# Turning the 32x32 blocks of a triangular inverse on VectorE instead of TensorE, in the recurrent part of a diffusion layer

## The chip, the cores and the metric

The kernel runs on one core of one Trainium2 chip. The metric is device time in microseconds, from the first to the last instruction of one execution and the little that lies around it. The time of before is the median of three runs.

## The reference, cut to what matters

One layer of a hybrid backbone is applied to 128 prompt tokens and 512 sample tokens (640 columns in all). A combined input projection feeds a differential attention, a recurrent branch that runs over the tokens in both directions, and gates. A residual normalisation and a convolutional feed-forward block follow. The recurrent branch is what the change is about:

```python
def rwkv7_scan(s0, r, w, k, v, a, b, reverse):
    def step(S, inp):
        r_t, w_t, k_t, v_t, a_t, b_t = inp
        sa = jnp.einsum('bhvk,bhk->bhv', S, a_t)
        S = S * w_t[:, :, None, :] + sa[..., None] * b_t[:, :, None, :] + v_t[..., None] * k_t[:, :, None, :]
        return S, jnp.einsum('bhvk,bhk->bhv', S, r_t)
    s_final, ys = lax.scan(step, s0, xs, reverse=reverse)
```

There are 8 heads of 64, two directions, and 640 tokens. The final states of the prompt are an output (`new_s`).

## The kernel before, in words

The scan is done in chunks of 64 tokens: 10 chunks, 2 directions. Heads go in pairs, `i` = 0 to 3, and a pair has 2 heads x 2 directions x 10 chunks = 40 small systems. Each is a unit lower triangular 64x64 matrix that has to be inverted. The tile `MS` holds all 40 of a pair, with the 64 rows on partitions 0 to 63; partitions 64 to 127 hold other products.

One pair goes through these functions, which issue their work in the order written:

- `rw_b(i)` makes decays, keys and queries (VectorE, ScalarE, GpSimd); it is a generator, and is stepped from within `rw_m(i - 1)`.
- `rw_c(i)` multiplies keys with queries (L642) and masks the products into `MS` (L648, L651, VectorE).
- `rw_d(i)`, a generator, transposes values and keys and makes `UV` (L665, L677, L686, with evacuations on ScalarE).
- `rw_i(i)` inverts the two 32x32 diagonal blocks of each of the 40 systems. TensorE turns the blocks so that a system lies on a partition: 64 small matmuls against the identity (L706; the profile lists two instructions for each, 128 a pair) into PSUM, and four copies (L710) into `X`, whose 104 partitions are 40 systems' first blocks, 24 unused rows, and 40 systems' second blocks. Then 30 steps of forward substitution run on VectorE, each a product (L716) and a sum (L718). Then `X` is turned back by 8 transposes of TensorE (L729) and 16 copies (L733, 8 on VectorE, 8 on ScalarE) into `MS`.
- `rw_m(i)` joins the blocks (a transpose by VectorE, L741, and small matmuls L747, L755), turns, solves and joins the chunk transitions (`turned`, `solved`, `joined`: L777, L792, L813, L816) in ten iterations, with the chain of states in `step` (L839). At its end it turns the final states `FS` (L864), copies them out (L865) and stores them (L867).
- `rw_e(i)` makes the outputs (L888) and copies them out of PSUM (`y`, L889). `rw_f(i)`, a generator, normalises and gates them (L899 to L923) and stores them (L925).

PSUM banks for all of this come from `bank(psR, "m", 2)`, two banks in turn.

In between, TensorE is given products of the combined input projection, which do not depend on the recurrence: the generator `flow` yields one dense product at a time (L215, 128x128 weights, 320 columns), 38 blocks of 48 products after those done at the start, 1824 in all. `pull(n)` issues `n` of them. Weights are loaded by SyncE (L183), cast by ScalarE (L186), and their low part is taken by GpSimd (L187). `side()` steps the first generator in the list `sides` until it is finished, then the next. While `order[0]` is set, all of TensorE's instructions of this part are chained in the order in which they are issued. What is left of `flow` after `rw_f(3)` is issued in one go (`while pull(1)`).

After that comes attention: its loads of queries and keys (L1097) stand behind the store of `rw_f(3)` (L925) in SyncE's queue, and its first matmuls are L1116.

Of the kernel before, what the change touches and what calls it, by code (L numbers as in the profile page):

```python
# [11 lines left out]
F32 = mybir.dt.float32  # L12
F32R = mybir.dt.float32r
AF = mybir.ActivationFunctionType
ALU = mybir.AluOpType
# [3 lines left out]
P = 128  # L19
# [47 lines left out]
def tile_layer(ctx, tc, x_prompt, x_sample, cache_k, cache_v, state_rwkv, c, c_ctx, w_ada, b_ada, w_in,  # L67
# [4 lines left out]
    nc = tc.nc  # L72
    def chain(prev, bi):
        if prev is not None:
            tc.add_manual_dep(bi.ins, prev.ins.name,
                              mybir.DependencyInfo(mybir.DependencyClass.NoSync, mybir.DependencyReason.DATA),
                              reason="psum group order")
        return bi
# [114 lines left out]
    def pq(bi):  # L193

        if order[0]:
            order[1] = chain(order[1], bi)
        return bi
# [60 lines left out]
    def bank(pool, tag, bufs=1):  # L258
        return pool.tile([P, 512], F32, name="ps_" + tag, tag=tag, bufs=bufs)
# [18 lines left out]
    with tc.tile_pool(name="start", bufs=1) as sp, tc.tile_pool(name="psS", bufs=2, space=PSUM) as psS:  # L278
# [95 lines left out]
        prev = None  # L374
# [78 lines left out]
    def side(n=1):  # L453

        while sides and n:
            n -= 1
            if next(sides[0], None) is None:
                del sides[0]

    def need(i, key):  # L460
        while key not in R[i] and pull(1):
# [231 lines left out]
    def rw_i(i):  # L693
        MS = R[i]["MS"]

        X = rp.tile([104, 32, 32], F32, name="X", tag="st")
        tmp = rp.tile([104, 256], F32, name="tmpx", tag="tmpx")
        nc.gpsimd.memset(X[32:64], 0.0)
        prev = None

        for y in range(2):
            ps = bank(psR, "m", 2).rearrange("p (t s) -> p t s", s=32)
            for t in range(16):
                for b in range(2):
                    rows = slice(32 * b, 32 * b + 32)
                    prev = chain(prev, pq(nc.tensor.matmul(ps[64 * b:64 * b + 40, t, :], MS[rows, :, 32 * b + 16 * y + t], ident[rows, rows], start=True, stop=True)))  # L706
                if t % 8 == 7:
                    pull(6)
            for b in range(2):
                (nc.scalar.copy if b else nc.vector.tensor_copy)(out=X[64 * b:64 * b + 40, 16 * y:16 * y + 16, :], in_=ps[64 * b:64 * b + 40])  # L710
        Xf = X.rearrange("p t s -> p (t s)")
        nc.vector.memset(Xf[:, ::33], 1.0)
        for j in range(1, 31):
            n = 31 - j
            tv = tmp[:, 0:j * n].rearrange("p (t r) -> p t r", r=j)
            nc.vector.tensor_tensor(out=tv, in0=X[:, j:j + 1, 0:j].broadcast_to([104, n, j]),  # L716
                                    in1=X[:, j + 1:32, j:j + 1].broadcast_to([104, n, j]), op=ALU.mult)
            nc.vector.tensor_tensor(out=X[:, j + 1:32, 0:j], in0=X[:, j + 1:32, 0:j], in1=tv, op=ALU.add)  # L718
            side()
            pull(4)  # L720
        while "d_in" not in R[i]:
            side()
            pull(4)

        for y in (1, 0):
            ps = bank(psR, "m", 2)
            for u in (3, 2, 1, 0):
                c0 = 128 * (4 * y + u)
                prev = chain(prev, pq(nc.tensor.transpose(out=ps[:, 104 * u:104 * u + 104], in_=Xf[:, c0:c0 + 128], identity=ident[0:104, 0:104])))  # L729
            for q in range(4):  # L730
                for b in range(2):
                    t0 = 32 * b + 16 * y + q
                    (nc.scalar.copy if b else nc.vector.tensor_copy)(  # L733
                        out=MS[32 * b:32 * b + 32, :, t0:t0 + 13:4],
                        in_=ps[32 * q:32 * q + 32, 0:416].rearrange("p (u r) -> p r u", u=4)[:, 64 * b:64 * b + 40, :])
        pull(16)

    def rw_m(i):
        AR, BT, UV, gs, st_in, MS = (R[i][k] for k in ("AR", "BT", "UV", "gs", "st_in", "MS"))
# [103 lines left out]
        for v in range(10):  # L843
            put = turned(v + 1) if 0 < v < 4 else None
            if v == 0:
                turned(0)()
                pull(10)
                put = turned(1)
            if 1 <= v <= 5:
                joined(v - 1)  # L850
            if v < 5:
                solved(v)
            if put:
                put()
            if v > 2:
                s = v - 3
                step([(d, cc, ST[:, d, cc + 1 - 2 * d, :]) for d, cc in ((0, 2 + s), (1, 9 - s))] +
                     ([(0, 1, FS[:, 0, :]), (1, 0, FS[:, 1, :])] if v == 7 else []))
            side(3)
            pull(14)  # L860
        ps = bank(psR, "m", 2)
        fo = rp.tile([64, 2, P], F32, name="fo", tag="tmpx")
        for d in range(2):
            pq(nc.tensor.transpose(out=ps[0:64, d * P:(d + 1) * P], in_=FS[:, d, :], identity=ident))  # L864
        nc.scalar.copy(out=fo, in_=ps[0:64, 0:256].rearrange("p (d k) -> p d k", d=2))  # L865
        for d in range(2):
            nc.sync.dma_start(out=new_s[d, 2 * i:2 * i + 2].rearrange("e v k -> v e k"), in_=fo[:, d, :].rearrange("p (e k) -> p e k", e=2))  # L867

        R[i].update(UV=UV, ST=ST)

    def rw_e(i):
        AR, MS, UV, ST = (R[i][k] for k in ("AR", "MS", "UV", "ST"))
        gup = cb.tile([P, P], F32, name="gup", tag="gup", bufs=1)
        nc.sync.dma_start(out=gup, in_=rw_g_up[:, i * P:(i + 1) * P])

        y = ft("y")
        for c0, n in ((0, 2), (2, 8)):
            ps = bank(psR, "m", 2)

            vals = [(d, cc, 0) for cc in range(c0, c0 + n) for d in range(2)]  # L880
            states = [(d, cc, 1) for cc in range(c0, c0 + n) for d in range(2) if (d, cc) not in ((0, 0), (1, 1))]
            todo = vals + states
            prev = None
            for z, (d, cc, kind) in enumerate(todo):
                for e in range(2):
                    hs = slice(64 * e, 64 * e + 64)
                    w, x = (ST[hs, d, cc, :], AR[d][hs, cc, 1, :]) if kind else (UV[:, e, d, cc, :], MS[:, e * 20 + d * NCH + cc, 64:128])
                    prev = chain(prev, pq(nc.tensor.matmul(ps[hs, (cc - c0) * 64:(cc - c0) * 64 + 64], w, x, start=z == 0, stop=z == len(todo) - 1)))  # L888
            nc.scalar.copy(out=y[:, c0 * 64:(c0 + n) * 64], in_=ps[:, 0:n * 64])  # L889
        R[i].update(y=y, gup=gup)  # L890

    def rw_f(i):
        v, bon, gup, y = (R[i][k] for k in ("v", "bon", "gup", "y"))
# [142 lines left out]
    for i in range(4):  # L1036
        if i:
            rw_e(i - 1)
        rw_c(i)
        need(i, "v_in")  # L1040
        sides.append(rw_d(i))
        if i:
            sides.append(rw_f(i - 1))
        rw_i(i)
        if i < 3:
            need(i + 1, "rk_in")
            sides.append(rw_b(i + 1))
        rw_m(i)
        while sides:
            side()  # L1050
            pull(3)
# [544 lines left out]
```

## Time and profile before

| | |
|---|---|
| time, median of 3 runs | 1432.46 us (1431.22 to 1436.12) |
| the profiled execution's own time | 1437.26 us |
| its span | 1435.2 us |
| mean granted clock of TensorE | 0.932 of 2.4 GHz |
| TensorE matmul busy | 1287.7 us (90%) |
| VectorE busy | 911.8 us (64%) |
| ScalarE, GpSimd busy | 563.7 us, 564.9 us (39% each) |

The profile is of one execution; its span ends with the last instruction, and 2.1 us of its time lie around it. Busy TensorE time is modelled from pipelined matmuls, so two dense products that are each listed with 0.31 us can start 0.15 us apart. A row of the timeline is: start, duration (both us), engine, line, operation, output<-inputs, shape, count, and in brackets the idle time of the engine just before and what ended it. The recurrent part lies between 69 and 711 us of the span.

### The profile page before, as it was taken

What the parts mean: (1) busy time and instruction counts of PE and PEld (TensorE: products, weight loads), DVE (VectorE), ACT (ScalarE), POOL (GpSimd) and SP (SyncE); (2) the same over time, 40 slices, a digit from 0 to 9 for tenths busy, and PEclk for the clock granted to TensorE, in tenths of its full rate; (3) what the DMA queues carried; (4) which work ended last, traced back from release to release, by engine and by line L of the source; (5) the groups of instructions that cost most, each with busy time, mean ns of one, the idle gap of its engine ahead of it and who ended that gap; (6) DMA issues with size and microseconds to landing.
All of it is one profiled execution on the core that took longest, in us unless ns stands there. A gap on an engine that the chain in (4) does not pass through costs nothing.

```text
span 1435.2 us, 27691 instructions
## 1 busy us (share of the span) xinstructions
PE 1287.7 (90%) x11105; PEld 1140.6 (79%) x11105; DVE 911.8 (64%) x1683; ACT 563.7 (39%) x1158; POOL 564.9 (39%) x424
## 2 busy tenths in 40 slices
PE   6998898988888999999979889968999999999994
PEld 5887887877777888889867777758988989989983
DVE  2365847584847563831266523597897987778777
ACT  3442533344324441533355412354543433434432
POOL 3252217331643232212220235546654735536623
PEclk9997998898988998999989999978999999999997
DMA  9411212220222111212656787513232232322222
GB/s 306 125 49 34 63 30 69 78 76 28 64 72 70 51 33 51 77 50 75 195 160 204 265 265 265 171 60 102 74 104 73 74 96 66 90 66 79 69 67 88
DMA packets 157459, 144.64 MB, mean 101 GB/s; under 512 B 10490, under 2 KB 128020, under 8 KB 157332
## 3 DMA queue, kind: packets, MB, share of 16 engines
q1 hardware_dynamic: 147490, 127.85, 29.0%
q10 hardware_dynamic: 9842, 15.03, 3.1%
q8 instruction: 87, 1.43, 0.4%
q14 instruction: 40, 0.33, 0.1%
HBM read 121.06 MB, written 19.69 MB: 98 GB/s over the span
## 4 chain that ended last, share of the span: by engine, by line
PE 38%; DVE 16%; issue 5%; POOL 4%; ACT 3%; DMA 2%; SPq 0%; ACTq 0%; DVEq 0%; POOLq 0%
PE ps_d L1413 8%; PE ps_d L215 6%; PE ps_x L215 4%; PE ps_e L1413 3%; PE acc L1449 2%; PE acc L1447 2%; PE acc L1448 2%; DVE sums L1386 2%; DVE zacc L1462 1%; PE acc L1249 1%; PE T L1140 1%; POOL wl L224 1%; DMA ws<-in_w_out_dram 1%; DVE X L718 1%; DVE tmpx L716 1%
## 5 line engine op out<-in xcount | busy, mean ns | idle before, releaser
L187 POOL TENSOR_TENSOR wl<-ws,wh 128x512 fp32r<-128x512 f32 x100 | 138.5, 1386 | 400.5 <-ACT wh L186 349.4
L224 POOL TENSOR_TENSOR wl<-sums,wh 128x512 fp32r<-128x512 f32 x88 | 137.4, 1568 | 38.3 <-ACT wh L223 36.5
L1413 PE MATMUL ps_d<-oph,wh 128*128 128x320 f32 x440 | 138.5, 315 | 10.6 <-DVE u L1425 5.0
L224 POOL TENSOR_TENSOR wl<-wu,wh 128x512 fp32r<-128x512 f32 x63 | 88.9, 1412 | 142.9 <-ACT wh L223 129.6
L1413 PE MATMUL ps_d<-oph,wl 128*128 128x320 f32 x440 | 137.5, 313 | 0.6 <-POOL wl L224 0.6
L1413 PE MATMUL ps_d<-opl,wh 128*128 128x320 f32 x440 | 137.3, 312 | 0.7 <-DVE opl L224 0.7
L186 ACT CAST wh<-ws 128x512 fp32r<-128x512 f32 x100 | 61.4, 618 | 171.3 <-PE ps_d L215 66.9
L215 PE MATMUL ps_x<-hl,wh 128*128 128x320 f32 (+1 forms) x304 | 104.5, 344 | 0.0
L215 PE MATMUL ps_x<-hh,wh 128*128 128x320 f32 (+1 forms) x304 | 104.5, 344 | 0.0
L215 PE MATMUL ps_x<-hh,wl 128*128 128x320 f32 (+1 forms) x304 | 104.2, 343 | 0.0
L215 PE MATMUL ps_d<-hl,wh 128*128 128x320 f32 (+1 forms) x304 | 103.7, 341 | 0.0
L215 PE MATMUL ps_d<-hh,wl 128*128 128x320 f32 (+1 forms) x304 | 103.6, 341 | 0.0
L215 PE MATMUL ps_d<-hh,wh 128*128 128x320 f32 (+1 forms) x304 | 103.4, 340 | 0.0
L1413 PEld LDWEIGHTS ps_d<-oph,wh 128*128 128x128 f32 x440 | 83.7, 190 | 15.1 <-ACT wh L223 7.7
L1413 PEld LDWEIGHTS ps_d<-opl,wh 128*128 128x128 f32 x440 | 83.7, 190 | 2.0 <-POOL hf L1343 1.1
L1413 PEld LDWEIGHTS ps_d<-oph,wl 128*128 128x128 f32 x440 | 83.7, 190 | 1.4 <-POOL wl L224 1.2
L223 ACT CAST wh<-sums 128x512 fp32r<-128x512 f32 x88 | 54.6, 620 | 65.2 <-PE ps_e L1413 25.4
L1447 PE MATMUL acc<-wh,gh 128*128 128x512 f32 x195 | 77.5, 398 | 2.6 <-ACT gh L223 2.6
L1448 PE MATMUL acc<-wl,gh 128*128 128x512 f32 x195 | 77.3, 397 | 0.0
L1449 PE MATMUL acc<-wh,gl 128*128 128x512 f32 x195 | 76.1, 397 | 0.5 <-DVE gl L224 0.5
L223 ACT CAST wh<-wu 128x512 fp32r<-128x512 f32 x63 | 39.1, 621 | 73.2 <-PE acc L1449 30.1
L215 PEld LDWEIGHTS ps_x<-hh,wh 128*128 128x128 f32 x304 | 63.4, 209 | 2.6 <-issue 1.1
(439 smaller groups left out, 3641.2 us busy)
## 6 DMA issues: line engine op xcount, KB each, us to landing
wu<-in_w_up_dram SPq DMA_DIRECT2D x42, 512.0 KB
ws<-in_w_in_dram SPq DMA_DIRECT2D x76, 256.0 KB
wa<-in_w_ada_dram SPq DMA_DIRECT2D x24, 512.0 KB
ws<-in_w_down_dram SPq DMA_DIRECT2D x44, 256.0 KB
wa<-in_w_ada_dram SPq DMA_DIRECT2D x8, 1024.0 KB
ks<-qk_dram SPq DMA_DIRECT2D x32, 192.0 KB
g_dram<-tg ACTq DMA_DIRECT2D x16, 320.0 KB
tg<-g_dram SPq DMA_DIRECT2D x16, 320.0 KB
```

The lines of the kernel that those rows point to most:

```text
L186: nc.scalar.copy(out=wh, in_=ws)
L187: (lo_eng or nc.gpsimd).tensor_tensor(out=wl, in0=ws, in1=wh.bitcast(F32), op=ALU.subtract)
L215: pq(nc.tensor.matmul(pd, w[:, k, :], x[:, g, sl], start=g == 0 and z == 0, stop=g == kb - 1 and z == 2))
L223: nc.scalar.copy(out=hi, in_=src)
L224: (lo_eng or nc.vector).tensor_tensor(out=lo, in0=src, in1=hi.bitcast(F32), op=ALU.subtract)
L716: nc.vector.tensor_tensor(out=tv, in0=X[:, j:j + 1, 0:j].broadcast_to([104, n, j]), in1=X[:, j + 1:32, j:j + 1].broadcast_to([104, n, j]), ...
L718: nc.vector.tensor_tensor(out=X[:, j + 1:32, 0:j], in0=X[:, j + 1:32, 0:j], in1=tv, op=ALU.add)
L1386: (nc.vector if q in USM else nc.gpsimd).tensor_tensor(out=o, in0=x0, in1=x1, op=op)
L1413: nc.tensor.matmul(ps, w[:, k, :], x[:, b, k, :], start=k == 0 and z == 0, stop=k == 3 and z == 2)
L1447: nc.tensor.matmul(acc, a_h, wh, start=first, stop=False)
L1448: nc.tensor.matmul(acc, a_h, wl, start=False, stop=False)
L1449: nc.tensor.matmul(acc, a_l, wh, start=False, stop=last)
```

## The change

The blocks go to `X` and back by VectorE's own 32x32 transposes. `X` now has 128 partitions in four groups of 32: the first blocks of systems 0 to 31 and of 8 to 39, and the second blocks of the same. Systems 8 to 31 are thus worked twice, with equal results, and written back twice. The transposes read `MS` with a step of 128 elements (512 bytes) from element to element of a row, and write it so on the way back. There are 8 of them in a pair, 32 in all. The matmuls L706 and L729 and the copies L710 and L733 go, and so does GpSimd's memset of unused rows.

`side()` steps the generators in turn. The final states are turned, copied and stored at the end of `rw_e(i)` instead of at the end of `rw_m(i)`. And more dense products are issued at some places: 32 instead of 24 while the blocks are turned, 26 instead of 16 behind the inverse, 16 instead of 14 in each of the ten iterations of `rw_m`, and 40 new ones ahead of `rw_c(0)`.

```diff
         while sides and n:
             n -= 1
-            if next(sides[0], None) is None:
-                del sides[0]
+            f = sides.pop(0)
+            if next(f, None) is not None:
+                sides.append(f)
...
-        X = rp.tile([104, 32, 32], F32, name="X", tag="st")
-        tmp = rp.tile([104, 256], F32, name="tmpx", tag="tmpx")
-        nc.gpsimd.memset(X[32:64], 0.0)
-        prev = None
-
-        for y in range(2):
-            ps = bank(psR, "m", 2).rearrange("p (t s) -> p t s", s=32)
-            for t in range(16):
-                for b in range(2):
-                    rows = slice(32 * b, 32 * b + 32)
-                    prev = chain(prev, pq(nc.tensor.matmul(ps[64 * b:64 * b + 40, t, :], MS[rows, :, 32 * b + 16 * y + t], ident[rows, rows], start=True, stop=True)))
-                if t % 8 == 7:
-                    pull(6)
-            for b in range(2):
-                (nc.scalar.copy if b else nc.vector.tensor_copy)(out=X[64 * b:64 * b + 40, 16 * y:16 * y + 16, :], in_=ps[64 * b:64 * b + 40])
-        Xf = X.rearrange("p t s -> p (t s)")
-        nc.vector.memset(Xf[:, ::33], 1.0)
+        X = rp.tile([P, 32, 32], F32, name="X", tag="st")
+        tmp = rp.tile([P, 256], F32, name="tmpx", tag="tmpx")
+        turns = [(X[32 * g:32 * g + 32], MS[32 * (g // 2):32 * (g // 2) + 32, 8 * (g % 2):8 * (g % 2) + 32, 32 * (g // 2):32 * (g // 2) + 32].rearrange("p c t -> p t c")) for g in range(4)]
+        for x, m in turns:
+            nc.vector.transpose(out=x, in_=m)
+            pull(8)
+        nc.vector.memset(X.rearrange("p t s -> p (t s)")[:, ::33], 1.0)
...
-        for y in (1, 0):
-            ps = bank(psR, "m", 2)
-            for u in (3, 2, 1, 0):
-                c0 = 128 * (4 * y + u)
-                prev = chain(prev, pq(nc.tensor.transpose(out=ps[:, 104 * u:104 * u + 104], in_=Xf[:, c0:c0 + 128], identity=ident[0:104, 0:104])))
-            for q in range(4):
-                for b in range(2):
...
-        pull(16)
+        for x, m in turns:
+            nc.vector.transpose(out=m, in_=x)
+        pull(26)
...
             side(3)
-            pull(14)
-        ps = bank(psR, "m", 2)
-        fo = rp.tile([64, 2, P], F32, name="fo", tag="tmpx")
-        for d in range(2):
-            pq(nc.tensor.transpose(out=ps[0:64, d * P:(d + 1) * P], in_=FS[:, d, :], identity=ident))
-        nc.scalar.copy(out=fo, in_=ps[0:64, 0:256].rearrange("p (d k) -> p d k", d=2))
-        for d in range(2):
-            nc.sync.dma_start(out=new_s[d, 2 * i:2 * i + 2].rearrange("e v k -> v e k"), in_=fo[:, d, :].rearrange("p (e k) -> p e k", e=2))
-
-        R[i].update(UV=UV, ST=ST)
+            pull(16)
+        R[i].update(UV=UV, ST=ST, FS=FS)
...
         R[i].update(y=y, gup=gup)
+        FS = R[i]["FS"]
+        ps = bank(psR, "m", 2)
+        fo = rp.tile([64, 2, P], F32, name="fo", tag="tmpx")
...
     for i in range(4):
         if i:
             rw_e(i - 1)
+        else:
+            pull(40)
         rw_c(i)
```

## Rows read from the trace of the kernel before

**Rows 1.** The page's part 1: engine, busy us, share of the span, instructions.
```profile
PE 1287.7 (90%) x11105; PEld 1140.6 (79%) x11105; DVE 911.8 (64%) x1683; ACT 563.7 (39%) x1158; POOL 564.9 (39%) x424
```

**Rows 2.** Windows: length, busy PE PEld DVE ACT POOL, clock, DMA share, GB/s.
```profile
125.20:174.90 49.70, 44.71 (x430) 41.99 (x433) 35.42 (x84) 24.57 (x51) 10.09 (x8) 0.86 0.17 51
...
265.50:328.50 63.00, 51.64 (x456) 46.66 (x457) 47.06 (x98) 26.12 (x54) 21.69 (x16) 0.85 0.24 74
...
421.50:479.70 58.20, 51.01 (x458) 45.79 (x459) 41.06 (x93) 25.88 (x55) 16.75 (x12) 0.91 0.20 63
...
561.70:613.70 52.00, 48.70 (x457) 44.93 (x459) 34.44 (x86) 23.36 (x50) 10.99 (x8) 0.90 0.20 63
613.70:664.30 50.60, 48.88 (x808) 44.51 (x809) 15.72 (x51) 17.14 (x40) 8.95 (x7) 0.97 0.19 59
664.30:711.30 47.00, 46.24 (x428) 44.47 (x426) 7.31 (x22) 14.52 (x33) 14.12 (x11) 1.00 0.46 138
```

**Rows 3.** Timeline of TensorE, pair 0.
```profile
125.21 1.31 PE L706 MATMUL ps_m<-ident,MS 32*40 32x32 f32 x32 [0.45 <-DVE MS L648]
...
153.08 0.31 PE L215 MATMUL ps_x<-hh,wl 128*128 128x320 f32 x1
153.23 0.31 PE L215 MATMUL ps_x<-hh,wh 128*128 128x320 f32 x1
```

**Rows 4.** Timeline of VectorE, pair 0, from the last masking to the joining.
```profile
124.47 0.68 DVE L648 TENSOR_TENSOR MS<-ps_ch,mk 128x512 f32<-128x512 f32 x1
...
136.65 0.18 DVE L716 TENSOR_TENSOR tmpx<-X 104x30 f32<-104x30 f32 x1 [0.69 <-issue]
...
136.86 0.21 DVE L718 TENSOR_TENSOR X<-X,tmpx 104x30 f32<-104x30 f32 x1
...
166.20 0.19 DVE L718 TENSOR_TENSOR X<-X,tmpx 104x30 f32<-104x30 f32 x1
...
173.21 1.50 DVE L741 STREAM_TRANSPOSE Y<-MS 32x1280 f32<-32x1280 f32 x1
```

**Rows 5.** Groups by line on VectorE, 60 to 712 us: busy us, mean ns of one.
```profile
L733 DVE COPY MS<-ps_m 32x160 f32<-32x160 f32 x32 | 13.3, 434 | 10.8 <-PE ps_m L729 5.3 <-ACT MS L733 4.8
...
L741 DVE STREAM_TRANSPOSE Y<-MS 32x1280 f32<-32x1280 f32 x4 | 6.0, 1497 | 0.1
L710 DVE COPY X<-ps_m 40x512 f32<-40x512 f32 x8 | 5.5, 683 | 26.9 <-PE ps_m L706 26.9
...
L749 DVE COPY Vt<-ps_m 32x320 f32<-32x320 f32 x8 | 3.9, 483 | 4.4 <-PE ps_m L747 2.6 <-ACT Vt L749 1.8
```

**Rows 6.** Waits of TensorE, 125 to 711 us: total us, times, longest us.
```profile
PE ps_m L747 <- DVE Y L741: 8.8, 4, 4.1
PE ps_m L888 <- ACT fo L865: 7.1, 2, 4.1
PE ps_ch L839 <- DVE ST L841: 4.6, 4, 2.2
...
PE ps_m L729 <- DVE X L718: 2.7, 1, 2.7
```

**Rows 7.** Timeline of TensorE in the first pair's masking.
```profile
114.54 0.79 PE L642 MATMUL ps_m<-AR,BK 64*128 64x128 f32 x2 [6.08 <-DVE MS L648]
```

**Rows 8.** Timeline, all engines, from the last outputs to attention.
```profile
669.79 0.59 ACT L889 COPY y<-ps_m 128x512 f32<-128x512 f32 x1 [3.76 <-PE ps_m L888]
...
678.80 1.95 POOL L517 TENSOR_TENSOR rn<-rn,mhalf 128x10 f32<-128x10 f32 x1 [1.16 <-DVE rn L515]
...
692.80 0.55 DVE L923 SCALAR_TENSOR_TENSOR yc<-yc,vT,ps_m 128x320 f32<-128x320 f32 x1 [0.31 <-PE ps_m L922]
...
696.90 1.65 SPq L1097 DMA_DIRECT2D qs<-qk_dram  x2
...
702.65 2.50 SPq L1097 DMA_DIRECT2D ks<-qk_dram  x4
...
710.48 1.10 PE L1116 MATMUL S<-ks,qs 128*128 128x320 f32 x7 [0.76 <-ACT pt L1121]
```

More of the change, by code (lines that the diff above doesn't have):

```diff
@@ L715, in rw_i @@
             tv = tmp[:, 0:j * n].rearrange("p (t r) -> p t r", r=j)
-            nc.vector.tensor_tensor(out=tv, in0=X[:, j:j + 1, 0:j].broadcast_to([104, n, j]),
-                                    in1=X[:, j + 1:32, j:j + 1].broadcast_to([104, n, j]), op=ALU.mult)
+            nc.vector.tensor_tensor(out=tv, in0=X[:, j:j + 1, 0:j].broadcast_to([P, n, j]),
+                                    in1=X[:, j + 1:32, j:j + 1].broadcast_to([P, n, j]), op=ALU.mult)
             nc.vector.tensor_tensor(out=X[:, j + 1:32, 0:j], in0=X[:, j + 1:32, 0:j], in1=tv, op=ALU.add)
@@ L723, in rw_i @@
             pull(4)
-        for y in (1, 0):
-            ps = bank(psR, "m", 2)
-            for u in (3, 2, 1, 0):
-                c0 = 128 * (4 * y + u)
-                prev = chain(prev, pq(nc.tensor.transpose(out=ps[:, 104 * u:104 * u + 104], in_=Xf[:, c0:c0 + 128], identity=ident[0:104, 0:104])))
-            for q in range(4):
-                for b in range(2):
[L732 to L735, printed above, removed]
-        pull(16)
+        for x, m in turns:
+            nc.vector.transpose(out=m, in_=x)
+        pull(26)
     def rw_m(i):
@@ L890, in rw_e @@
         R[i].update(y=y, gup=gup)
+        FS = R[i]["FS"]
+        ps = bank(psR, "m", 2)
+        fo = rp.tile([64, 2, P], F32, name="fo", tag="tmpx")
+        for d in range(2):
+            pq(nc.tensor.transpose(out=ps[0:64, d * P:(d + 1) * P], in_=FS[:, d, :], identity=ident))
+        nc.scalar.copy(out=fo, in_=ps[0:64, 0:256].rearrange("p (d k) -> p d k", d=2))
+        for d in range(2):
+            nc.sync.dma_start(out=new_s[d, 2 * i:2 * i + 2].rearrange("e v k -> v e k"), in_=fo[:, d, :].rearrange("p (e k) -> p e k", e=2))
     def rw_f(i):
```

## The prediction

> **What bounds the kernel now.** I read the page's busy shares first. TensorE is the engine with the most to do, and no other comes near it [rows 1]. But the change touches only the recurrent part (69 to 711 us), so I went on to the windows of that part and then to the waits and timelines inside it. In the four windows from the last masking of a pair to its joining (L747), TensorE's busy time is well below the length, and its mean granted clock is 0.85 to 0.91, so a share of each window ran at 1.2 GHz and not at 2.4 [rows 2]. A dense product starts 0.15 us after the one before at full clock [rows 3]; 174 of them go into each of these windows (24 + 120 + 16 + 14 by the code), which is 26 us of 50 to 63. The rest is turning blocks, waiting, and small products. The reader is to see that in these windows VectorE's chain sets the end. The blocks are masked until 125.15 us, the first step of substitution starts only at 136.65, the last ends at 166.39, and VectorE's transpose for the joining starts at 173.21 [rows 4]. So 11.5 us pass before the 30 steps and 6.8 us behind them, on trips through TensorE, PSUM and two copying engines. The list of TensorE's waits names the same places: the joining waits on that transpose (8.8 us in four), the outputs wait on the copy of the final states (7.1 us in two), the chain of states on its sums (4.6 us) [rows 6].
>
> What is left of the dense products is used at the end: TensorE has no idle time to speak of from 664.3 to 711.3 us [rows 2]. By the code's counts 224 of the 1824 are still there behind the last `rw_m`: 12 + 112 cover `rw_e` and `rw_f` of the last pair, and 100 run in one go behind them.
>
> **The change part by part.** The profiled execution took 1437.3 us (span 1435.2 and 2.1 around it); that is 4.8 above the median of the runs, and I take the same difference for the forecast.
>
> *The turning of the blocks.* L706 costs TensorE four times 1.31 us a pair [rows 3], 21 us in all, and L729 some 3 more. They go. VectorE loses, per pair, two copies of 0.683 and eight of 0.434 us, 4.8 us [rows 5], and gets eight transposes. Their price is not in the trace in this form. The nearest row is L741: 1280 elements a partition in 1.497 us [rows 5]. An instruction on 30 elements takes 0.19 [rows 4], so about 0.16 is fixed and 1.04 ns an element is left; 1024 elements are 1.23 us. L741, though, reads 32 neighbours in a row, and the new ones step over 512 bytes at each element, reading on the way there and writing on the way back. The first step of substitution bears on this: L716 reads 30 elements 128 bytes apart and takes 0.18, L718 writes 30 so apart and takes 0.21, against 0.19 for 30 neighbours [rows 4]. That shows nothing for reading, and about 0.7 to 1.0 ns an element for writing. L733 agrees: it writes 160 elements with gaps in 0.434 us where L749 writes 320 neighbours in 0.483 [rows 5]; at L749's 1.0 ns an element 160 would be 0.32, so 0.11 us or 0.7 ns an element is extra. I take 1.23 us for a transpose to `X` and 1.23 + 0.87 = 2.10 us for one back. Per pair: 4 x 1.23 + 4 x 2.10 = 13.3 us. The bounds are 9.8 us (no step costs anything) and 4 x 2.3 + 4 x 2.3 = 18.4 us (1.0 ns more both ways).
>
> [...]
>
> VectorE's busy time in the four windows is 35.4, 47.1, 41.1 and 34.4 us [rows 2]. With 4.8 taken off and 13.3 put on it is 43.9, 55.6, 49.6 and 42.9, together 192. TensorE's work there becomes 192 dense products (32 + 120 + 26 + 14), 28.4 us, and some 6 to 10 us of small ones, which is less. So VectorE sets these windows, and with a microsecond each for hand-overs they are 196 us against 222.9 now: **-27**. Bounds: -41 at 9.8 us a pair, -7 at 18.4. What is late next is the joining L747, which still waits for L741 on VectorE, with 40 dense products (6 us) as cover. The alternation in `side()` moves no work: `rw_d` and `rw_f` need 28 steps together and the loop has 30; `rw_d` ends at step 25 instead of 13, still before the transposes back, and each generator's matmuls now lie 8 products apart instead of 4. I cost it at nothing; without that room in the loop the `while "d_in"` behind it would add a step of 0.6 us each.
>
> *40 products ahead of `rw_c(0)`.* They take 40 x 0.148 = 5.9 us and stand ahead of a wait of 6.08 us on VectorE [rows 7]: **0**, and they cost 5.9 if VectorE is ready sooner.
>
> *Two more in each of 40 iterations of `rw_m`.* 80 x 0.148 = 11.8 us. The waits that they can hide are those on the chain of states, 4.6 us in the one row [rows 6], and its neighbours. The last pair's `rw_m` is nearly all TensorE (48.9 busy of 50.6) [rows 2] and hides nothing. I take half hidden: **+6**, between +4 and +12.
>
> *Final states behind the outputs.* The 7.1 us of waiting go: the third bank that TensorE asks for was the one with the final states, and ScalarE's in-order queue was late with it [rows 6]. Now the first masking product of the next pair asks for the bank of the second half of the outputs at once, and waits for its copy: 0.59 us [rows 8] and some 0.3 for hand-over, three times, and about 1 more where ScalarE is held up. **-3.5**, between -7 and 0. The two stores move behind the load of `gup` and ahead of the state loads of `rw_c` in SyncE's queue; the buffer that they read is next written by the first step of substitution, behind the whole of `rw_c` and the transposes, so I see nobody wait for them.
>
> *The end.* All pulls together issue 40 + 4 x 38 = 192 more products early, so 32 of 224 are left behind the last `rw_m`: 12 and then 20 in `rw_f`, nothing behind. The outputs take 5 us. Then `rw_f` is a chain of hand-overs: the copy 0.59, means, squares, GpSimd's power 1.95, spread, scale, gate, the last 0.55 [rows 8]; from its rows I estimate 10 us of work and a quarter of a microsecond for each of some dozen hand-overs, with the 32 products partly between: 15.5 us. That puts its end 20.5 us after the last `rw_m`, 29 us in the trace now. Attention's loads stand behind its store: from the first query load at 696.90 to the last key load's issue at 705.15 are 8.3 us [rows 8], and some 2 for landing. Then attention is where it now is at 711, after 20.5 + 10.5 + 1.5 for a start at 1.2 GHz = 32.5 us, against 47.0: **-14.5**, between -20 (loads placed ahead of the store) and -6. The dense products that were taken out were 28 us, so 14 of these 28 become idle time.
>
> Sum: -27 + 0 + 6 - 3.5 - 14.5 = **-39 us**, 1398 on the profiled execution's scale and **1393** for the median.
>
> **The rivals.** *Every step of 512 bytes costs, reading too.* All 32 transposes at 2.3 us: 32 x 2.3 instead of 53.3 is 20 more on VectorE's chain, -19 in all, 1413. [...] Against: L716's 0.18 us.
>
> *The gain is given back.* The windows shrink, but ScalarE's or VectorE's in-order queue holds TensorE up elsewhere (the densest work of query and key heads now falls into the first `rw_m`, beside `rw_b`), and the last pair runs bare for longer than 32.5 us. If the end is -6, `rw_m` +12 and the outputs 0, -27 leaves -21; 15 more of such waits, as many as L747 and L888 show together [rows 6], and -6 is left: 1428.
>
> *Slower.* VectorE's transposes are the bound at a higher price: the windows follow VectorE, so each 0.1 us more for a transpose is 3.2 us. From 39 / 32 = 1.2 us more than my mean of 1.67 on, that is from 2.9 us for one transpose (2.7 ns an element), the change loses; at 3.2 us it is 1443. For it: nothing but that the form is new. Against: the dearest step that the rows show, in writing, comes to about 2 ns an element.
>
> *Better.* Transposes at 1.23 us both ways (-14) and attention's loads ahead of the store (-6): 1373.
>
> **How the numbers follow.** Forecast 0.60, own range 1380 to 1405. Rival 1: 0.17. Rival 2: 0.10. Slower: 0.05. Better: 0.08. The range takes in the forecast, the better case, rival 1 and a part of rival 2: 1370 to 1422. A measurement of this kernel tells 0.3%, 4.3 us, from no change; forecast, rival 1, better and a few of rival 2 are faster by more: 0.88, same 0.06, slower 0.06.
>
> **What would show it.** The profile after should have 32 transposes at 1.2 and 2.1 us; windows from masking to joining of about 45, 56, 50 and 44 us with TensorE waiting at L747; no wait of L888 on the copy of final states, and short ones of L642 on the copy of outputs; dense products that run out in `rw_f(3)`, idle TensorE behind, and attention some 32 us after the last `rw_m`. I am wrong if the transposes cost much more than that, if VectorE doesn't set the windows (then TensorE's 35 to 40 us would, and the gain is larger), or if the queues behind ScalarE make new waits of 15 us and more.

## The result

| | median | ratio to before (95% interval) |
|---|---|---|
| before, in the same comparison | 1434.29 us | 1 |
| after | 1418.56 us | 0.9882 (0.9839 to 0.9925) |
| after, timed a second time beside later kernels | 1419.08 us | 0.9866 (0.9841 to 0.9892) |

The change makes the kernel 16 to 19 us faster. The forecast was 39 us, and 1393 for the median. The measured 1418.6 lies inside the stated range, but in the part of it that was meant for the rivals. The profiled execution spans 1419.0 us, 16.2 less than before.

### The profile after

Part 1 of the page, as in [rows 1]:

```profile
PE 1252.3 (88%) x10561; PEld 1110.0 (78%) x10561; DVE 952.8 (67%) x1675; ACT 544.5 (38%) x1118; POOL 562.7 (40%) x420
```

VectorE's groups between 60 and 712 us, as in [rows 5] (busy us, mean ns of one, idle before):

```profile
L701 DVE STREAM_TRANSPOSE X<-MS 32x1024 f32<-32x1024 f32 x16 | 31.7, 1982 | 0.2
L716 DVE STREAM_TRANSPOSE MS<-X 32x1024 f32<-32x1024 f32 x16 | 31.2, 1950 | 0.5
```

The transposes cost nearly the same both ways, 1.98 and 1.95 us. Going to `X` they were forecast at 1.23 us, coming back at 2.10. Now the four windows from the last masking to the joining, as in [rows 2], and the four stretches between them, from each joining to the next pair's last masking (of the last pair, to its outputs). The columns are those of [rows 2], and PEclk is the granted share of TensorE's full clock. First the windows after:

```profile
126.20:178.30 52.10, 36.92 (x305) 35.30 (x303) 49.94 (x85) 21.59 (x43) 10.84 (x8) 0.89 0.17 49
281.00:332.30 51.30, 42.74 (x334) 39.77 (x333) 48.24 (x94) 22.83 (x46) 15.25 (x11) 0.95 0.21 61
423.70:478.00 54.30, 43.00 (x330) 39.59 (x330) 49.63 (x92) 21.71 (x45) 11.58 (x9) 0.93 0.18 52
566.20:615.20 49.00, 43.02 (x338) 39.37 (x340) 45.92 (x85) 19.14 (x41) 11.97 (x9) 0.97 0.21 67
sum 206.70, PE 165.69 PEld 154.04 DVE 193.72 ACT 85.27 POOL 49.63; mean PE 41.42 PEld 38.51 DVE 48.43 ACT 21.32 POOL 12.41
```

Then the stretches between, before:

```profile
174.90:265.50 90.60, 81.77 (x1118) 70.84 (x1118) 53.86 (x102) 31.26 (x69) 39.83 (x30) 0.89 0.19 55
328.50:421.50 93.00, 81.26 (x1113) 71.23 (x1113) 55.70 (x103) 32.00 (x69) 43.33 (x32) 0.88 0.19 57
479.70:561.60 81.90, 76.37 (x1111) 66.48 (x1111) 43.53 (x96) 30.05 (x64) 25.83 (x19) 0.96 0.15 44
613.70:664.70 51.00, 49.28 (x812) 44.67 (x812) 15.72 (x51) 17.14 (x40) 8.95 (x7) 0.97 0.19 59
sum 316.50, PE 288.68 PEld 253.22 DVE 168.81 ACT 110.45 POOL 117.94; mean PE 72.17 PEld 63.30 DVE 42.20 ACT 27.61 POOL 29.49
```

and after:

```profile
178.30:281.00 102.70, 89.10 (x1144) 78.48 (x1145) 59.34 (x107) 32.29 (x70) 48.29 (x36) 0.86 0.23 69
332.30:423.70 91.40, 85.00 (x1146) 74.66 (x1147) 57.74 (x107) 33.96 (x74) 47.48 (x34) 0.90 0.23 73
478.00:566.20 88.20, 83.71 (x1135) 73.98 (x1136) 40.34 (x91) 28.45 (x63) 26.44 (x20) 0.89 0.16 49
615.20:667.70 52.50, 51.55 (x830) 47.22 (x830) 15.90 (x52) 18.32 (x44) 11.14 (x9) 0.97 0.24 73
sum 334.80, PE 309.37 PEld 274.34 DVE 173.32 ACT 113.01 POOL 133.36; mean PE 77.34 PEld 68.59 DVE 43.33 ACT 28.25 POOL 33.34
```

The windows are 16.3 us shorter than before (223.0), and VectorE is busy for 94% of them. But the stretches between them are 18.3 longer, with 20.7 us more of busy TensorE. The growth is uneven: 12.1 us in the first stretch, 6.3 in the third, 1.5 in the fourth, and the second is 1.6 shorter. So up to the end of the last `rw_m` nothing is gained: it ends at 667.7, before at 664.7. The gain, 19 us less these 3, comes from behind it. From there to the first turning of attention's weights, and from that to the first sum of the projections behind attention, after:

```profile
667.70:705.90 38.20, 24.19 (x239) 20.92 (x239) 8.25 (x23) 7.07 (x18) 4.92 (x4) 0.73 0.48 128
705.90:835.70 129.80, 115.07 (x837) 93.82 (x835) 70.31 (x151) 57.62 (x165) 22.18 (x18) 0.95 0.72 230
```

Before they were 49.0 and 137.4 us. TensorE's waits from the first window to the last outputs, as in [rows 6]:

```profile
PE ps_m L728 <- DVE Y L722: 22.4, 4, 11.7
...
PE ps_m L643 <- ACT y L862: 3.3, 3, 2.6
```

The wait of the joining has grown from 8.8 to 22.4 us. Its place in pair 0 is in TensorE's timeline:

```profile
166.37 0.31 PE L215 MATMUL ps_x<-hl,wh 128*128 128x322 f32 x1
178.34 1.29 PE L728 MATMUL ps_m<-Y,MS 32*32 32x32 f32 x80 [11.66 <-DVE Y L722]
...
180.00 0.47 PE L215 MATMUL ps_x<-hh,wh 128*128 128x320 f32 x1
180.26 0.47 PE L215 MATMUL ps_x<-hl,wh 128*128 128x320 f32 x1
```

The dense products run out at 166.7 and TensorE stands for 11.7 us. Behind that a dense product starts 0.27 us after the one before, and not 0.15 as in [rows 3]: TensorE runs at half its clock, here called 1.2 GHz (320 columns in 0.267 us are 1.2 a nanosecond). Windows around two of these places show the granted clock:

```profile
166.60:178.30 11.70, 0.08 (x1) 0.00 (x0) 11.46 (x11) 1.10 (x3) 0.35 (x1) 0.65 0.16 45
178.30:183.70 5.40, 5.36 (x96) 5.26 (x97) 1.95 (x4) 0.84 (x2) 0.00 (x0) 0.50 0.05 15
...
477.20:490.90 13.70, 12.04 (x208) 10.56 (x210) 3.13 (x7) 3.72 (x8) 2.52 (x2) 0.50 0.17 50
```

In the first row TensorE is idle and VectorE is busy for 11.46 of 11.70 us. In the second, right behind it, TensorE works without a pause at 0.50 of its clock, and in the third, around the joining of pair 2, at 0.50 too for 12.04 busy us of 13.70.

In the first stretch TensorE also waits for VectorE: for the states, for the joined matrices (`AR`) and for decays of the next pair (`gs`). Before, of these three only the states were waited for (L839), 0.7 us. The last line is what stands on VectorE just ahead of the sum that makes `AR`: the rotation of a finished query or key block, itself waiting for GpSimd.

```profile
PE ps_ch L820 <- DVE ST L822: 3.9, 2, 2.9
PE ps_m L530 <- DVE AR L802: 3.0, 1, 3.0
...
PE ps_ch L820 <- DVE gs L582: 2.1, 1, 2.1
```
```profile
205.44 0.69 DVE L956 TENSOR_TENSOR qkt<-qkt,sw 128x512 f32<-128x512 f32 x1 [1.15 <-POOL sw L921]
```

Four such blocks are finished in the first stretch, and two before.

### The profile page after: what moved, and what is told of

It is laid out like the page before. It is cut to its first block, busy times and chain, and to the rows that moved or that the text cites. A ratio compares the mean times of both kernels' runs of the same rounds, so it can differ in the third digit from the quotient of the medians.

```text
span 1419.0 us, 26512 instructions
## 1 busy us (share of the span) xinstructions
PE 1252.3 (88%) x10561; PEld 1110.0 (78%) x10561; DVE 952.8 (67%) x1675; ACT 544.5 (38%) x1118; POOL 562.7 (40%) x420
## 5 line engine op out<-in xcount | busy, mean ns | idle before, releaser
L215 PE MATMUL ps_x<-hh,wh 128*128 128x320 f32 (+1 forms) x304 | 101.5, 334 | 0.0
L1396 PEld LDWEIGHTS ps_d<-opl,wh 128*128 128x128 f32 x440 | 83.7, 190 | 2.0 <-POOL hf L1326 1.1
L1396 PEld LDWEIGHTS ps_d<-oph,wl 128*128 128x128 f32 x440 | 83.7, 190 | 1.4 <-POOL wl L224 1.2
L215 PEld LDWEIGHTS ps_d<-hh,wh 128*128 128x128 f32 x304 | 63.4, 209 | 2.6 <-issue 0.9
```

Of the source, the lines that this page charges most:

```text
L215: pq(nc.tensor.matmul(pd, w[:, k, :], x[:, g, sl], start=g == 0 and z == 0, stop=g == kb - 1 and z == 2))
L1396: nc.tensor.matmul(ps, w[:, k, :], x[:, b, k, :], start=k == 0 and z == 0, stop=k == 3 and z == 2)
```

## The experiments

Each run is given by its median and its ratio to the kernel before timed beside it. "Windows" and "between" are the sums of the four stretches shown above; in the kernel after they are 206.7 and 334.8, before 223.0 and 316.5.

**The parts alone.** First the transposes alone, in the kernel before, instead of TensorE's turning and the copies:

```diff
+        for x, m in turns:
+            nc.vector.transpose(out=x, in_=m)
+            pull(6)
...
+        for x, m in turns:
+            nc.vector.transpose(out=m, in_=x)
         pull(16)
```

> Only the turning by VectorE is put into the kernel before; the dense products stay at their old counts (6 at each of four places, 16 behind), the generators in their old order, the final states at their old place. In the profile after, a transpose costs 1.95 to 1.98 us either way and the four windows from masking to joining came to 206.7 us in place of 222.9. Theory: the windows are the whole gain of the change, VectorE sets them, and the rest of the change sums to about nothing: -16 us, between -20 and -12, windows of 205 to 210 us. The forecast's own step said -27 for this part: -24 or more would mean that the other parts cost time. Rival: with fewer dense products as cover the gain is lost elsewhere, in rw_m or at the end: -8 or less.

Measured: 1430.18 us, 0.9948 (0.9928 to 0.9968), 7.5 us less. Windows 214.1, between 315.9:

```profile
sum 214.10, PE 163.73 PEld 150.37 DVE 202.00 ACT 80.57 POOL 58.37; mean PE 40.93 PEld 37.59 DVE 50.50 ACT 20.14 POOL 14.59
```

VectorE's 202.0 us are what the forecast's own sum gives when a transpose costs 1.97: 192 + 62.9 - 53.3 = 201.6. The theory was wrong in that the windows give 9 us and not 16. The rival's size came, but not its cause: nothing is lost in `rw_m` (315.9 against 316.5) or at the end (48.9 against 49.0). And this run bears on what a wait at the joining does behind it. TensorE waits there for 26.4 us in four (the first row names the evacuation that VectorE does right behind the joining's transpose), more than the 22.4 of the kernel after:

```profile
PE ps_m L728 <- DVE bs L246: 14.9, 2, 12.9
PE ps_m L728 <- DVE Y L722: 11.5, 2, 7.8
```

Yet the stretches behind these waits are as long as before; the first, behind a wait of 12.9 us, takes 90.8 us, before 90.6.

Then the 192 earlier products alone:

```diff
-                    pull(6)
+                    pull(8)
...
-        pull(16)
+        pull(26)
...
-            pull(14)
+            pull(16)
...
+        else:
+            pull(40)
```

> Only the 192 dense products that are issued earlier are put into the kernel before; the blocks are still turned by TensorE. 192 x 0.148 = 28.4 us of TensorE's work move from behind the last rw_m to places in front of it. The forecast priced this at +6 for rw_m, 0 elsewhere and -14.5 at the end, so -8.5. Theory, from the profile after: in rw_m each product costs its full time and some more at half clock (+15 in all), in the windows two thirds of 72 products are hidden (+4), the end gives back 11: about +8, between 0 and +14. Rival: the cover is free nearly everywhere as the forecast had it, -8 or less.

Measured: 1423.40 us, 0.9908 (0.9885 to 0.9931), 13 us less. The theory fell, and the forecast's -8.5 was nearer. The stretches between are 10.8 longer (327.3). In sum that is nearly the full price of the products in `rw_m` (80 x 0.148 = 11.8), but 10.0 of it stand in the first stretch, whose 20 products are 3 us of work. TensorE's waits in that stretch are those of the kernel after, though here it hardly waits at the joining:

```profile
PE ps_ch L839 <- DVE ST L841: 4.2, 1, 4.2
PE ps_m L529 <- DVE AR L821: 2.8, 1, 2.8
PE ps_ch L839 <- DVE gs L581: 2.1, 1, 2.1
```

But the windows are 6.3 shorter (216.7), the end 11.4 and what follows up to the projections' first sum 6.8. In the windows VectorE has 149.4 us of work in place of 158.0. My reading is that dense blocks whose results VectorE evacuates are finished ahead of them; no run shows that apart.

The states alone (at the end of `rw_e` and no more of `rw_m`) with the order of the generators:

```diff
-            if next(sides[0], None) is None:
-                del sides[0]
+            f = sides.pop(0)
+            if next(f, None) is not None:
+                sides.append(f)
...
+        FS = R[i]["FS"]
+        ps = bank(psR, "m", 2)
+        fo = rp.tile([64, 2, P], F32, name="fo", tag="tmpx")
```

> Only the move of the final states behind the outputs and the stepping of the generators in turn are put into the kernel before. The forecast: -3.5 for the states and 0 for the order. Theory: TensorE's wait for the copy of the final states goes (7.1 us in the trace of before) and a wait for the copy of the outputs comes (3.3 us there after): 0 to -4. Rival: stepping in turn moves rw_f's and rw_b's work on VectorE between the windows and rw_m and changes the time by more than 5 us, either way.

Measured: 1441.86 us, 1.0026 (1.0007 to 1.0045), some 4 us more: neither gain nor zero. The stretches between are 5.7 longer (322.2), the windows as before (222.6). Undoing each in the kernel after should then give it back:

> The kernel after with one part undone: the final states are turned, copied and stored at the end of rw_m again, ahead of the outputs. In the run with states and sides alone the stretch from the joining of pair 0 to the masking of pair 1 was 3.4 us longer than before, where only the move of the states can matter, since just one generator is left there. Theory: the move costs 1 to 4 us in all and undoing it gives that back. The forecast said the move saves 3.5: then this kernel is 3 us or more slower than the kernel after. Third possibility: the difference was one of the order in which the planner puts the instructions, and nothing changes (within 1.5 us).

> The kernel after with the generators stepped as before, the first of the list until it is finished. Forecast: nothing (0). Theory, from the run with states and sides alone, which was 4 us slower than before: stepping in turn costs 0 to 3 us, since rw_f's steps for the pair before come to stand beside the substitution on VectorE, which sets the windows; undoing it gives that back. Rival: in turn is better, because rw_d is finished in time either way and rw_f is no longer left to the end: 3 us or more slower than the kernel after.

Measured: 1416.37 us, 0.9841 (0.9818 to 0.9864), and 1417.09 us, 0.9847 (0.9826 to 0.9867). Both intervals overlap those of the kernel after. Neither part moves the time measurably in the changed kernel; the three parts alone add up to -7.5 - 13 + 4 = -16.5.

**The step of 512 bytes.** Two kernels like the one after, but with transposes that read and write neighbours. The diff is that of the first; the second has `12 + 20 * (g % 2):20 + 20 * (g % 2)` for the systems:

```diff
-        turns = [(X[32 * g:32 * g + 32], MS[32 * (g // 2):32 * (g // 2) + 32, 8 * (g % 2):8 * (g % 2) + 32, 32 * (g // 2):32 * (g // 2) + 32].rearrange("p c t -> p t c")) for g in range(4)]
+        turns = [(X[32 * g:32 * g + 32], MS[32 * (g // 2):32 * (g // 2) + 32, 8 * (g % 2):8 * (g % 2) + 8, :].rearrange("p c (a t) -> p (c a) t", a=4)) for g in range(4)]
```

> The kernel after, but the transposes read and write 1024 neighbouring elements of a partition of MS, so the blocks that are inverted are not the right ones (the inverse is left out in that sense). Same count, same places, no step of 512 bytes. Theory: VectorE sets the windows and the step is what the forecast mis-sized: a transpose takes 1.2 us, each of four windows is 8 x 0.75 = 6 us shorter, the time is 24 us below the kernel after (between 18 and 28). Rival: the price is that of the transpose itself and not of the step: it still takes 1.9 us or more and the time is that of the kernel after. Second rival: the transposes fall to 1.2 us but another engine then sets the windows or the time is given back in rw_m: less than 12 us below the kernel after.

> As the run with flat transposes, but the 1024 neighbouring elements are those of systems 12 to 19 and 32 to 39, which the last two maskings write, so that no transpose can start before the masking ends (in the first run with flat transposes they did, and the windows fell by 33 us, of which the step of 512 bytes can only explain 24). The blocks that are inverted are again not the right ones. Theory: the step alone is worth 32 x 0.74 = 24 us on VectorE's chain; windows of 180 to 188 us, the time 16 to 24 us below the kernel after. Rival: with the early start gone, another engine or rw_m takes it back: less than 12 us.

Measured: 1396.04 us, 0.9714 (0.9693 to 0.9735), and 1392.89 us, 0.9679 (0.9655 to 0.9703); 26 us below the kernel after timed beside the second. In the first, transposes start ahead of the last maskings, and its windows are 171.3 (35 shorter; the expectation has 33), so the second is the one to read. The two transposes of the second kernel (lowest, median, highest ns) and its windows:

```profile
L701 DVE STREAM_TRANSPOSE X<-MS x16: 1222/1235/1239, 122.8 to 546.1; 32x1024 f32<-32x1024 f32 x16
L716 DVE STREAM_TRANSPOSE MS<-X x16: 1232/1234/1239, 160.9 to 581.2; 32x1024 f32<-32x1024 f32 x16
```
```profile
sum 181.50, PE 158.32 PEld 147.76 DVE 171.78 ACT 85.41 POOL 48.75; mean PE 39.58 PEld 36.94 DVE 42.95 ACT 21.35 POOL 12.19
```

The step costs 0.75 us of 1.98 a transpose reading and 0.72 writing, 23.4 us over 32. The windows are 25.2 shorter and the time follows. So VectorE sets these windows.

**Less on VectorE's chain.** Two transposes of a pair that can run ahead of the last maskings (the first lines), and in a second kernel the joining's own transpose ahead of two others too (the last lines):

```diff
+        turns = [(X[32 * g:32 * g + 32].rearrange("p t (e c) -> p t e c", e=2),
+                  MS[32 * (g % 2):32 * (g % 2) + 32, :, 32 * (g % 2):32 * (g % 2) + 32].rearrange("p (e c) t -> p t e c", e=2)[:, :, :, 4 * (g // 2):4 * (g // 2) + 16]) for g in range(4)]
...
+        for x, m in turns[0::2]:
+            nc.vector.transpose(out=m, in_=x)
+        Y11 = rp.tile([32, 40, 32], F32, name="Y11", tag="bk", bufs=2)
+        nc.vector.transpose(out=Y11, in_=MS[0:32, :, 0:32])
+        for x, m in turns[1::2]:
+            nc.vector.transpose(out=m, in_=x)
```

> The kernel after with the 32 systems of a transpose chosen otherwise: 0 to 15 and 20 to 35 in the first two, 4 to 19 and 24 to 39 in the other two, in place of 0 to 31 and 8 to 39. The last two maskings write systems 16 to 19 and 36 to 39, so the first two transposes don't need them and can run in the 1.2 us stretches in which VectorE waits for TensorE's products. The number of transposes and the step of 512 bytes stay. Theory: VectorE's chain sets the windows, and two of eight transposes, 2 x 1.97 us a pair, leave them in part: windows 2 to 4 us shorter each, 6 to 14 us below the kernel after. Rival: the transposes that run early hold up the last maskings on the same queue by what they take: no change.

> The early groups of the run before, and the transpose for the joining (1.50 us) is issued right after the two transposes back that it reads, ahead of those for the second blocks, which only the second product of the joining needs. Theory: the joining's first product starts 2 to 3.9 us earlier in each of four windows and VectorE's copies behind it wait in its queue, so half is left: 4 to 8 us below the run with early groups. Rival: the copies of the first product stand behind the transposes of the second blocks on VectorE, and nothing is gained.

Measured: 1414.94 us, 0.9836 (0.9816 to 0.9856), and 1414.83 us, 0.9836 (0.9808 to 0.9864). With early groups the windows fall by 4.7 to 202.0, with the stretches between as they were (335.1). With the early joining they fall by 3.8 more (198.2), and the stretches between grow by 4.1 (339.2). Both expectations were too high, and both intervals overlap that of the kernel after. Where the second gain went was not followed up.

**Where the 80 products of `rw_m` stand.** First at the end, where TensorE is idle:

```diff
-            pull(16)
+            pull(14)
```

> The kernel after with 14 instead of 16 dense products in each of the 40 iterations of rw_m; 80 products more are left behind the last rw_m, where TensorE stands idle for some 16 us. In the run with the earlier products alone, rw_m and what follows up to the next masking were 10.8 us longer for 80 products, 11.8 us of work. Theory: they are paid nearly in full in rw_m and the idle time at the end takes most of them: rw_m and its neighbours 8 to 11 us shorter, the end 2 to 6 us longer, the time 4 to 8 us below the kernel after. Rival: the 7 us that attention and the projections behind it gained come with the early products too, and are lost again: no change or slower.

Measured: 1423.98 us, 0.9899 (0.9876 to 0.9923): no gain. The stretches between are 11.2 us shorter (323.6), the first by 13.2 (89.5), where TensorE's three waits on VectorE shrink to one of 1.9, while the second is 8.1 longer (99.5). But the windows are 7.1 longer (VectorE has 200.5 us of work there again), and the end is 7.5 longer. The rival's cause is not it: the stretch through attention stays at 129.4. So I put them where TensorE waits for the joining, first with the early groups and then without:

```diff
-        pull(26)
+        pull(46)
...
-            pull(16)
+            pull(14)
```

> The early groups of the run before, with 46 instead of 26 dense products behind the inverse and 14 instead of 16 in each of the ten iterations of rw_m: 80 products move from rw_m to where TensorE waits for the joining's transpose (22 us in four windows in the profile after, 12 of them in the first). Theory: a product in rw_m costs its time and one at the wait does not: rw_m 9 to 11 us shorter, windows 0 to 5 longer, 4 to 10 us below the run with early groups. Rival: more of the queries' and keys' evacuations on VectorE fall into the windows with the products, as in the run with 14, and VectorE sets the windows: no gain.

> The kernel after with one change: 46 instead of 26 dense products behind the inverse and 14 instead of 16 in each iteration of rw_m; the groups of systems stay as in the kernel after. With early groups the same 80 products gave 10 us, and TensorE ran at 1.2 GHz for some 14 us less in rw_m and its neighbours. Theory: in rw_m the 80 products cost their time and the wait at the joining lets the clock fall for the start of rw_m; both go: 8 to 14 us below the kernel after, the same whichever groups are used. Rival: it needs the shorter windows of the early groups: less than 5 us.

Measured: 1404.65 us, 0.9767 (0.9743 to 0.9791), and 1401.25 us, 0.9765 (0.9740 to 0.9789). By the ratios that is 14 to 17 us below the kernel after, whichever groups are used, and they are the fastest kernels of the study that compute all of the reference. The profiled execution of the second, 1395.9 us, is the shortest of its five, and that of the kernel after the longest of its four, so the two profiles differ by more than the medians. Its stretches between:

```profile
177.00:269.40 92.40, 79.76 (x1120) 69.48 (x1120) 58.63 (x105) 31.39 (x69) 47.10 (x36) 0.93 0.24 74
320.30:411.90 91.60, 81.38 (x1126) 70.88 (x1127) 57.01 (x107) 33.58 (x73) 47.10 (x34) 0.87 0.23 72
465.30:543.00 77.70, 74.25 (x1115) 65.01 (x1116) 41.59 (x91) 28.29 (x63) 26.14 (x20) 0.98 0.18 55
593.00:643.50 50.50, 48.95 (x810) 44.43 (x809) 15.73 (x51) 17.15 (x40) 9.34 (x8) 0.97 0.23 70
sum 312.20, PE 284.35 PEld 249.80 DVE 172.96 ACT 110.40 POOL 129.68; mean PE 71.09 PEld 62.45 DVE 43.24 ACT 27.60 POOL 32.42
```

They are 22.6 us shorter than in the kernel after, while the windows grow by only 2.3 (209.0). With early groups it is 17.3 shorter (317.8 against 335.1) and 6.2 longer (208.2 against 202.0). TensorE's waits at the joining (L728), in the second kernel, are down to two rows. But in pair 0 it now stands a little earlier, for ScalarE (first row), and the first window is no shorter (54.7 against 52.1):

```profile
PE ps_d L936 <- ACT vt L929: 8.5, 1, 8.5
...
PE ps_m L728 <- DVE bs L246: 2.7, 1, 2.7
...
PE ps_m L728 <- DVE Y L722: 1.9, 1, 1.9
```

The second kernel and the one with 14 differ by the 80 products at the wait alone. Those make the stretches between 11.4 shorter (312.2 against 323.6), the windows 4.8 and the end 7.5, so about half of the 22.6 is that the products left `rw_m`, and half that they stand at the wait.

**What is left behind the last `rw_f`.** With 14 products in `rw_m`, but 1 and not 8 between the steps of the last `rw_f`:

```diff
     for _ in rw_f(3):
-        pull(8)
+        pull(1)
```

> The kernel with 14 dense products in rw_m (112 left behind the last rw_m), but 1 instead of 8 between two steps of the last rw_f, so that some 86 products are left behind it, as 100 are in the kernel before; in the kernel with 14 none are. In all runs with none left, the stretch from the first attention block to the first sum of the projections behind it took 129 to 132 us, in all with 100 left 137 to 138. Theory: what is left behind brings its weight loads and gate stores into attention's loads, and that stretch is 135 us or more again. Rival: the stretch depends on what was done earlier, not on the rest: 129 to 132 us, and only the stretch ahead of attention is longer.

Measured: 1422.69 us, 0.9924 (0.9897 to 0.9950). Its two stretches, to attention and through the projections' first sum, and those of the kernel with 14:

```profile
658.20:699.30 41.10, 34.47 (x319) 31.54 (x319) 9.69 (x25) 10.93 (x27) 9.67 (x8) 0.89 0.46 130
699.30:834.70 135.40, 117.86 (x834) 95.21 (x832) 70.31 (x151) 57.84 (x165) 21.48 (x18) 0.93 0.72 229
```
```profile
660.60:706.30 45.70, 33.05 (x319) 30.67 (x319) 8.66 (x25) 10.82 (x27) 9.60 (x8) 0.85 0.51 140
706.30:835.70 129.40, 113.83 (x834) 92.21 (x833) 70.27 (x151) 57.61 (x165) 22.17 (x18) 0.96 0.73 228
```

The second stretch is 6 us longer with products left behind, and attention starts 4.6 us sooner. So the end and this stretch have to be priced together, which the forecast did not do. That it is the late blocks' weight loads and stores that delay attention's loads was not shown apart.

The kernel after, timed again:

> The kernel after, unchanged, beside the others of this call: 1415 to 1420 us, a ratio to before of 0.985 to 0.989.

It is the third line of the table of results.

## Why the prediction was wrong

Its terms, on the profiled executions:

| term | forecast | measured |
|---|---|---|
| windows, masking to joining | -27 | -16.3 |
| 40 products ahead of the first masking | 0 | +1.0 |
| two more in each iteration of `rw_m`, and the states behind the outputs | +6 - 3.5 | +18.3 |
| the end, up to attention | -14.5 | -10.8 |
| attention and projections | 0 | -7.6 |
| all behind | 0 | -0.8 |
| sum | -39 | -16.2 |

**The step that failed: "I take half hidden: +6".** The 80 products were not half hidden. With 16 in place of 14 in each iteration the stretches between were 10.8 us longer in the kernel with the earlier products alone (against before; it has more of them in the windows too) and 11.2 in the kernel after (against the one with 14). The forecast was 6, between 4 and 12. And the stretches hold more than the products: they grew by 18.3. The prediction looked only at `rw_m`'s own waits, which it took as cover, and named a wait at the joining ("with TensorE waiting at L747") without asking what follows it. What the runs show of it, by stretch:

- In the first stretch (+12.1), 20 products are 3 us of work. The rest comes together with TensorE's waits on VectorE, 9.0 us in three rows where 0.7 were, and with finished query and key blocks, four instead of two. The kernel with the earlier products alone has the same (100.6 us, 9.1 of waits), so it needs neither the transposes nor the wait at the joining. It isn't shown that the blocks alone do it: the kernel with the products at the wait has four there too and takes 92.4.
- In the third (+6.3) TensorE is busy for 83.7 of 88.2 us, and the length goes with the clock. With 16 products it takes 88.2 us at a mean of 0.89 and 83.3 at 0.98 (earlier products alone); with 14, 84.2 at 0.93, 81.9 at 0.96 (before) and 77.7 at 0.98 (products at the wait).
- The clock doesn't set every stretch: the kernel after, profiled a second time, has 91.4 us in the second stretch again, at 0.94 instead of 0.90.

Over the four stretches the time at 1.2 GHz comes to 70 us after and 52 before (twice the part that is missing from a mean of 1; in slices of 0.25 us from 100 to 700 us the clock is 1.00 or 0.50 in 2363 of 2400, in either kernel). If work takes twice as long there, the extra 18 hold work that would take 9 at full clock, and 11.8 + 9 = 20.8 is about the 20.7 us by which TensorE's busy time rises. The twice is an estimate: a dense product starts 0.267 us after the one before instead of 0.148, 1.8 times. That is a sum of busy time, though, not of length, and a long wait at the joining doesn't bring it about by itself: with the transposes alone TensorE waits there longer and the stretches are as before. How the 7 us that the products don't explain divide between VectorE's queue, the clock and the move of the states with the generators' new order (5.7 us of stretches in the kernel before; nothing measurable when either is undone in the kernel after) stays open.

**"1.23 us for a transpose to `X`".** It costs 1.98, and one back 1.95 instead of 2.10, so all 32 come to 62.9 us instead of 53.3, 9.6 more. This is the first rival: the step costs in reading too. The row that spoke against it, the product L716 of the kernel before at 0.18 us, steps over 128 bytes and 30 elements; it did not carry to 512 bytes and 1024. In the trace reading and writing cost nearly the same at this step, 1.78 ns an element one way and 1.75 the other, (1982 - 160) / 1024 and (1950 - 160) / 1024 with the forecast's 160 ns of fixed time, against 1.05 for neighbours. The runs show this price, not what makes it. The forecast's 1.23 us for neighbours was right to 0.01.

**"A microsecond each for hand-overs".** VectorE is busy for 193.7 of 206.7 us, so 13.0 are not work, 3.2 a window; that is 9.0 of the 10.7 us by which the windows missed. That VectorE's work is still near the forecast's 192 is chance: 9.6 more for transposes, and 8 less in the windows with the earlier dense products (202.0 with transposes alone). That VectorE sets the windows was right.

**The final states.** The wait on their copy is gone and the new one on the outputs' copy is there, 3.3 us in three, as named. But undoing the move changes nothing that can be measured, so the -3.5 is 0.

**The end.** The dense products run out in the last `rw_f`, and attention's first turning comes 38.2 us after the last `rw_m`; before, it was 49.0. That is 3.7 us less gain than forecast. But the forecast stopped there, and 7.6 us more come in the stretch behind, which the run with 86 products left over has 6 us longer. So the term was too small: -18.4 in place of -14.5.

**The alternation** and the 40 products are near the 0 that was forecast: undoing the alternation changes nothing measurable, and the first masking ends 1.0 us later.

The second rival came nearest in kind: a gain given back between the windows, through VectorE's queue and the query and key blocks in the first `rw_m`. The rows of the first stretch are of that sort; the third stretch and the price of the products are not. Its sum of -6 gives 1426 and not 1428.

## What to carry to other kernels

Work that is moved as cover has a price at its new place: read there how long the engine waits and in which row, and put the work at that row. Here moving 80 products to the wait took 17 to 23 us off the stretches that had held them and put 2 to 6 on the windows in which TensorE waited. Price a stretch by what follows from the move too: in the first stretch here, 3 us of products came with finished blocks and 8 us more of waiting on VectorE. And don't put a longer stretch down to the wait ahead of it before a run shows it by itself: with the transposes alone, 26 us of waiting left the stretches as they were. And take a strided price only from a row with that stride and length.

## What was not expected of the hardware

A VectorE transpose of 32x1024 float32 elements takes 1.98 us reading and 1.95 us writing with a step of 512 bytes, and 1.23 us both ways with neighbours. TensorE, after 11.7 us without work, ran at 1.2 GHz (a granted clock of 0.50) for the first 5.4 us of the work that followed. In another pair it was at 0.50 for 13.7 us, of which 12.0 were busy.
